# Hybrid conv and pooling layers on one core: fewer weights split ahead, a third GpSimd tile cut at tap 20, and buffers for the first norm's squares

## The chip, the core and the metric

The kernel runs on one core of one Trainium2 chip. Its engines are TensorE (PE in the rows; PEld is its weight load), VectorE (DVE), ScalarE (ACT), GpSimd (POOL) and SyncE (SP), whose queue issues the transfers here. Each engine carries out its own instructions in the order in which the program lists them, and waits where an operand or a buffer is not ready. The metric is the device time of one launch in microseconds; before the change it is 744.97 us, the median of three runs.

## The reference

Two layers act on a latent stream x of 1024 tokens by 1024 channels. Neither layer needs the context stream (only a later kind of layer reads it). Both are gated by a condition c.

```python
# each layer: modulated RMS norm, mixer, gated residual
sh, sc, gt = split(silu(c) @ w_mod[i] + b_mod[i], 3)
h = rms(x, norm_g[i]) * (1 + sc) + sh
x = x + gt * mixer_i(h)

def conv_mixer(h):                      # layer 0
    a, b, g = split(h @ w_in, 3)
    y = a * sigmoid(b)
    y = depthwise_conv(y, dw, 31 taps, same padding) + db
    y = silu(layernorm(y, ln_g, ln_b)) * silu(g)
    return y @ w_out

def pool_mixer(h):                      # layer 1
    v, g = split(h @ w_in, 2)
    pooled = [window_mean(v_k, w) for k, w in enumerate((2, 4, 8, 16))] - v
    y = (grouped 256x256 matmuls of pooled) * scale
    return (y * silu(g)) @ w_out
```

All arrays are float32.

## The kernel before

Channels lie on the 128 partitions, tokens along the free dimension. Every 1024 x 1024 product is made of eight output tiles of 128 channels (`ct` or `m`), each a sum over eight input tiles (`kt`), for two halves of 512 tokens (`h`; in layer 1 the parts are 504 and 520 tokens).

*Products in three passes.* Each float32 operand is split into a high part in fp32r (`hi_part`, L166 and L167, on ACT) and the rest (`lo_part`, L171 and L172, on DVE, or on GpSimd where `eng=nc.gpsimd`). `mm3` (L221 to L223) adds high x high, high x low and low x high. So a group of one output tile and one half is 24 matmuls. A weight is loaded into one of four `raw` buffers and split into two of four `w` tiles; so two split weights can be there at a time, and the next cast waits until the group two before it has been used.

*Layer 0.* After the input and its norm, tiles `a` and `b` are made for `y`. The depthwise convolution (`conv`, `conv_taps`) takes 31 taps for each tile and half. For most tiles DVE accumulates in PSUM (L524). For the tiles in `POOL_CT` ACT multiplies (L511, into one of two `pr` buffers) and GpSimd adds to `z` (L512), tap by tap: two tiles in half 0, five in half 1. The gates `g` (names `wg<ct><h>`, `psg`, `sgw`) fill TensorE while the convolution goes on and while the norm is computed; they are stored in DRAM (`sgd`) and come back as `sgr`.

*Weights split ahead.* `split_ahead` loads weights of layer 1 (`wk<i>`), splits them on ACT and GpSimd and stores the parts in DRAM (`keep`, names `kw<i>`). `load_pl` later loads such parts instead of splitting again (`load_kept`), or loads and splits the weight on ACT and DVE where none are kept. Each such weight is 512 KB, its two parts 1 MB.

*Norm and output.* `layernorm(h)` sums the eight `z` tiles on TensorE (`mr`), spreads the mean (`mu`), subtracts it on DVE, squares on ACT (`sqz`) and sums the squares on TensorE (`vpz`). For half 0 `square_sums` (L296) streams one column against each block of the square; for half 1 `quarter_sums` (L311) streams the square against 32 columns of ones. Squares lie in two `sq` buffers. `rstd_rows` makes the power on GpSimd (L268) and spreads it (`rbz`). `gate_norm` makes `y1`, and `out_half` the output product (`pso`), the residual and the sums for layer 1's norm (`vpy`, `rby`). `h2_half` makes layer 1's input (`h20`, L660 on DVE, L167 on ACT, L172 on DVE).

*What sets the order.* The program is written once and a scheduler orders the instructions of each engine by their priorities and a model of their times. `behind([...])` keeps what is issued inside it behind the given instructions in their engine's order, without a wait. `conv` has a low priority, so its taps fill gaps. In half 1 the tiles 4 to 7 are issued inside `behind([h2_done])`, where `h2_done` is DVE's last `lo_part` of layer 1's input.

*The second half's gates.* `gate_g(ct, (0, 1))` in the loop over `FILL` and `CORD[:2]` makes both halves of gates 0 and 2 with one load; gates 1 and 3 keep their weight (`wg_last`) and make half 1 after `layernorm(0)`; gates 4 to 7 load theirs again while layer 1's input is made.

Of the kernel before, what the change touches and what calls it, by code (L numbers as in the profile page):

```python
# [17 lines left out]
KT = 8  # L18
# [8 lines left out]
CORD = [ct for p in PAIRS for ct in p]  # L27
FILL = (4, 6, 5, 7)
MIX_AT = 4
ASIDE = (2, 3, 10, 11, 4, 5, 12, 13, 6, 7, 14, 15)  # L30
AT = (2, 2, 2, 2, 2, 2)
EARLY_W = (1, 1, 2, 2)
EARLY_AT = (0, 2, 1, 1)
EARLY_ENG = ((0, 0, 0, 0), (1, 1, 1, 1))
# [2 lines left out]
HOLD = (4, 2, 3, 4)  # L37
LAST = 2
MID_OUT = 6
TAIL = 8  # L40
NA = HW - TAIL
NB = L - NA
# [13 lines left out]
def hybrid_kernel(ctx, tc, xT, vecs, wm, wk, cv_first, cv_w, cv_wo, pl_w, pl_grp, pl_wo, out):  # L56
# [29 lines left out]
    def half(tag, name, dt=F32, cols=HW):  # L86
        return S.tile([P, WIDTH.get(tag, HW)], dt, tag=tag, name=name, bufs=RINGS[tag])[:, :cols]
# [4 lines left out]
    def bank(tag, name):  # L92
        return PS.tile([P, HW], F32, tag=tag, name=name, bufs={"mm": 5, "ax": 1, "cv": 2}[tag])
# [7 lines left out]
    def hs(h):  # L101
        return slice(h * HW, (h + 1) * HW)
# [4 lines left out]
    def packed(tags, name):  # L107
        res = []
        for j, tag in enumerate(tags):
            u = unit(tag, f"{name}{j}")  # L110
            res += [u[:, hs(0)], u[:, hs(1)]]
        return res
# [51 lines left out]
    def hi_part(hi, src, add=None):  # L164
        if add is None:
            return nc.scalar.copy(hi, src)  # L166
        return nc.scalar.activation(hi, src, AF.Identity, bias=add)  # L167
# [15 lines left out]
    @contextmanager  # L183
    def behind(instructions):
        with ExitStack() as stack:
            for i in instructions:
                stack.enter_context(tc.issue_after(i.ins))
            yield
# [104 lines left out]

        return (sums, None), add

    def square_sums(xs, name, vp):  # L296


        def add(i):
            sq = half("sq", f"sq{name}{i}")  # L300
            done = nc.scalar.activation(sq, xs[i], AF.Square)
            for j in range(4):
                nc.tensor.matmul(
                    vp[:, j : j + 1], sq[:, bl(j)], ones[:, 0:1], start=i + j == 0, stop=i == KT - 1,
                    skip_group_check=True,
                )
            return done

        return (None, vp), add

    def quarter_sums(xs, name, vp):  # L311


        def add(i):
            sq = half("sq", f"sq{name}{i}")
            done = nc.scalar.activation(sq, xs[i], AF.Square)
            for j in range(4):
                nc.tensor.matmul(
                    vp[32 * j : 32 * j + 32, :P], ones[:, :32], sq[:, bl(j)], start=i == 0, stop=i == KT - 1
                )  # L320
            return done

        return ("quarters", vp), add
# [36 lines left out]
    xs = [None, None]  # L360
# [106 lines left out]
    gt0, sh1, a1, gt1 = (const.tile([P, KT], F32, name=n) for n in ("gt0", "sh1", "a1", "gt1"))  # L467
# [19 lines left out]
    def conv(h, ct, taps=None, count=None):  # L487

        with priority(LATER * (1 + h)):
            for _ in islice(taps or conv_taps(h, ct), count):  # L490
                pass
# [59 lines left out]
    def gate_g(ct, halves, after=(), start=KT // 2, wg=None):  # L551
        wg = wg or gate_w(ct, halves[0])
        for h in halves:
            ps = mmps(f"psg{ct}{h}")
            gemm(ps, wg, hT[h], after, start)
            s = half("sg", f"sgw{ct}{h}")
            nc.scalar.activation(s, ps, AF.Silu)
            i = CORD.index(ct)
            nc.sync.dma_start(out=sgd[h][i // 2][:, hs(i % 2)], in_=s)
# [4 lines left out]

    aside = list(ASIDE)
    for i, ct in enumerate((*FILL, *CORD[:2])):
        split_ahead(AT[i])
        gate_g(ct, (0,) if ct in FILL else (0, 1))
    wg_last = {ct: gate_w(ct, 0) for ct in CORD[2:4]}
    for ct in CORD[2:4]:  # L570
        gate_g(ct, (0,), wg=wg_last[ct])
# [3 lines left out]
    def layernorm(h):  # L575
        z = [zs[h][ct] for ct in CORD]
        sums = axps(f"mr{h}")
        row = S.tile([P, HW], F32, tag="row", name=f"mrow{h}", bufs=1)
        mu = axps(f"mu{h}")
        with priority(-LATER):  # L580
            for i, ct in enumerate(ZORD[h]):
                g = slice(32 * (i % 4), 32 * (i % 4) + 32)
                nc.tensor.matmul(sums[g, :], onesd[:, :32], zs[h][ct], start=i < 4, stop=i >= 4)
            nc.scalar.copy(row, sums)
            last = nc.tensor.matmul(mu, selm, row, start=True, stop=True)
        sums_done[h] = last
        total, add = (square_sums, quarter_sums)[h](z, f"z{h}", bank(("ax", "cv")[h], f"vpz{h}"))
        for i in range(KT):
            nc.vector.tensor_tensor(out=z[i], in0=z[i], in1=mu, op=ALU.subtract)
            with priority(-LATER):  # L590
                squared[h] = add(i)
        return z, *rstd_rows(total, f"z{h}")
# [28 lines left out]
    def out_half(h, y1, ws, done, beside=None):  # L621
# [27 lines left out]
            finish(m, ps)  # L649
        return x1, total  # L650

    def h2_half(h, x1, total, region, first):
        rb, rb_done = rstd_rows(total, f"y{h}")
        res = []
        for kt in range(KT + 1):
            if kt < KT:
                if kt % 2 == 0:
                    u = pair(region, first + kt, f"h2{h}{kt}")
                x = x1[kt]
                mul = nc.vector.scalar_tensor_tensor(  # L660
                    out=x, in0=x, scalar=a1[:, kt : kt + 1], in1=rb, op0=ALU.mult, op1=ALU.mult
                )
                if kt:
                    ordered(mul)
                else:
                    started = mul
                res.append(cut(u, hs(kt % 2)))
                hi_part(res[kt][0], x, sh1[:, kt : kt + 1])
            if kt:
                end = ordered(lo_part(*res[kt - 1], x1[kt - 1], sh1[:, kt - 1 : kt]))  # L670
        return res, started, end, rb_done
# [1 line left out]
    ws = [load_split(cv_wo[m], f"wo0{m}", ("Q", 2 * m), eng=nc.gpsimd) for m in range(3)]  # L673
    conv(1, 0)
    z, rb, rb_done = layernorm(0)
    gate_g(CORD[2], (1,), wg=wg_last[CORD[2]])
    gate_g(CORD[3], (1,), [rb_done], HOLD[0], wg_last[CORD[3]])
    y1, done = gate_norm(0, z, rb)
    conv(1, 1)
    conv(1, 3)  # L680
# [1 line left out]
    x1, total = out_half(0, y1, ws, done)  # L682
# [8 lines left out]
    h2_0, h2_started, h2_done, rb_done = h2_half(0, x1, total, "Q", 0)  # L691
# [159 lines left out]
    for g in range(4):  # L851
        group = layer1_group(g, 0, h2_0, early, group if g else None)
        if g == 0:
            with behind([h2_done]):
                for ct in range(4, KT):
                    conv(1, ct)
        if g:
            ahead += [load_split(pl_wo[m], f"wp{m}0", ("E", 2 * m)) for m in ((0,), (1,), (2, 3))[g - 1]]
    with priority(-LATER):
        z, rb, rb_done = layernorm(1)  # L860
    layer1_out(0, range(MID_OUT - 1), ahead, group)
    with behind(spread_done):
# [12 lines left out]
    x1, total = out_half(1, y1, ws, done, beside)  # L875
    h2_1, _, _, rb_done = h2_half(1, x1, total, "Y", 2)
# [57 lines left out]
```

## Time and profile before

| | |
|---|---|
| median of three runs | 744.97 us (744.68 to 745.39) |
| the profiled execution | 746.58 us, span of its instructions 744.8 us |
| TensorE | 718.7 us busy (96%) |
| DVE, GpSimd, ACT | 506.1, 452.4, 386.6 us busy |
| granted TensorE clock | 0.997 of full speed over the span |
| moved through DMA | 130.86 MB |

In the rows below, a timeline row gives start and length in us, the engine, the line, the operation, output<-input by the program's names with buffer numbers left out, and in brackets the idle time before it with what ended it. "x8" means that many instructions in a row, merged into one length. Matmul lengths overlap, since matmuls are pipelined; their starts tell the pace. The fp32 matmuls of the sums are recorded as two passes each.

### The profile page before, as it was taken

What the parts mean: (1) busy time and instruction counts of PE and PEld (TensorE: products, weight loads), DVE (VectorE), ACT (ScalarE), POOL (GpSimd) and SP (SyncE); (2) the same over time, 40 slices, a digit from 0 to 9 for tenths busy, and PEclk for the clock granted to TensorE, in tenths of its full rate; (3) what the DMA queues carried; (4) which work ended last, traced back from release to release, by engine and by line L of the source; (5) the groups of instructions that cost most, each with busy time, mean ns of one, the idle gap of its engine ahead of it and who ended that gap; (6) DMA issues with size and microseconds to landing.
All of it is one profiled execution on the core that took longest, in us unless ns stands there. A gap on an engine that the chain in (4) does not pass through costs nothing.

```text
span 744.8 us, 9979 instructions
## 1 busy us (share of the span) xinstructions
PE 718.7 (96%) x3574; PEld 568.7 (76%) x3574; DVE 506.1 (68%) x712; ACT 386.6 (52%) x577; POOL 452.4 (61%) x389
## 2 busy tenths in 40 slices
PE   3899999999999999999989999999999999999998
PEld 1677787676776788878756887778887888888997
DVE  6997998789899770579859976352646464377321
ACT  5365456656656575876776773353434432443110
POOL 2000889999999999899999992044217423343231
PEclk9999999999999999999999999999999999999999
DMA  8882006465788974543662165365725511234142
GB/s 323 323 325 83 0 1 248 154 249 210 276 343 288 336 301 183 190 139 110 210 215 83 57 218 192 141 222 192 237 95 207 186 47 42 86 114 142 57 130 73
DMA packets 43394, 130.86 MB, mean 176 GB/s; under 512 B 4816, under 2 KB 6992, under 8 KB 43344
## 3 DMA queue, kind: packets, MB, share of 16 engines
q1 hardware_dynamic: 43344, 130.22, 49.5%
q8 instruction: 28, 0.46, 0.2%
q14 instruction: 22, 0.18, 0.1%
HBM read 105.04 MB, written 25.17 MB: 175 GB/s over the span
## 4 chain that ended last, share of the span: by engine, by line
PE 73%; POOL 10%; DMA 7%; DVE 5%; ACT 2%; issue 2%; SPq 0%; POOLq 0%; DVEq 0%; ACTq 0%
POOL z L512 9%; PE psv L223 4%; PE psv L222 4%; PE psf L223 4%; PE psf L221 4%; PE psq L223 4%; PE psf L222 4%; PE psv L221 4%; PE psq L222 4%; PE psq L221 4%; PE ps L221 3%; PE ps L223 3%; PE ps L222 3%; PE psg L223 3%; PE psg L221 2%; PE psg L222 2%
## 5 line engine op out<-in xcount | busy, mean ns | idle before, releaser
L512 POOL TENSOR_TENSOR z<-z,pr 128x512 f32<-128x512 f32 (+8 forms) x210 | 292.0, 1392 | 35.0 <-ACT z L508 14.9
L511 ACT ACTIVATE pr<-y,VT 128x512 f32<-128x512 f32 (+8 forms) x210 | 150.2, 720 | 93.3 <-POOL z L512 88.4
L524 DVE SCALAR_TENSOR_TENSOR cv<-y,VT,cv 128x512 f32<-128x512 f32 (+9 forms) x261 | 175.2, 742 | 0.3
L820 DVE SCALAR_TENSOR_TENSOR xf<-psf,gt,xf 128x260 f32<-128x260 f32 (+1 forms) x24 | 13.3, 570 | 41.2 <-PE psf L223 37.1
L268 POOL TENSOR_TENSOR vrx<-vex,mhalf 128x4 f32<-128x4 f32 x2 | 2.1, 1026 | 56.2 <-ACT vex L266 56.2
L803 DVE SCALAR_TENSOR_TENSOR q<-psy,VT,q 128x260 f32<-128x260 f32 (+1 forms) x24 | 13.6, 571 | 30.8 <-PE psy L223 30.6
L613 DVE TENSOR_TENSOR z<-z,rbz 128x512 f32<-128x512 f32 x16 | 10.7, 679 | 30.1 <-PE rbz L274 30.1
L716 DVE TENSOR_TENSOR s<-v 128x535 f32<-128x535 f32 x8 | 12.3, 1538 | 19.5 <-ACT v L769 19.5
L166 ACT CAST y<-q 128x504 fp32r<-128x504 f32 (+1 forms) x16 | 9.9, 620 | 24.2 <-DVE q L803 24.2
L327 DVE SCALAR_TENSOR_TENSOR wmb<-wmb,s_row 128x1024 f32<-128x1024 f32 x16 | 19.3, 1218 | 0.0
L714 DVE TENSOR_TENSOR s<-v,psv 128x512 f32<-128x512 f32 x8 | 5.5, 682 | 20.1 <-ACT v L769 20.1
L339 PE MATMUL gv<-wk,srep 128*32 128x256 f32 x256 | 18.6, 388 | 0.0
L729 POOL TENSOR_TENSOR s<-s,ecol 128x1 f32<-128x1 f32 (+5 forms) x14 | 4.4, 311 | 22.5 <-DVE s L720 22.5
L720 DVE TENSOR_TENSOR s<-s 128x517 f32<-128x517 f32 (+5 forms) x24 | 17.5, 731 | 0.6
L629 DVE SCALAR_TENSOR_TENSOR xr<-pso,gt,xr 128x512 f32<-128x512 f32 x16 | 11.6, 743 | 8.1 <-PE pso L223 8.1
L605 ACT ACTIVATE gn<-z,VT 128x512 f32<-128x512 f32 x16 | 12.4, 776 | 9.2 <-DVE z L613 9.0
L529 DVE TENSOR_TENSOR z<-z,cv 128x512 f32<-128x512 f32 x9 | 6.2, 685 | 15.0 <-ACT z L528 15.0
L223 PE MATMUL psy<-pd,grs 128*128 128x260 f32 (+1 forms) x48 | 15.3, 319 | 0.0
L222 PE MATMUL psy<-pd,grs 128*128 128x260 f32 (+1 forms) x48 | 15.2, 318 | 0.0
L221 PE MATMUL psy<-pd,grs 128*128 128x260 f32 (+1 forms) x48 | 15.2, 320 | 0.0
L769 ACT COPY v<-psv 128x512 f32<-128x512 f32 x16 | 9.3, 582 | 10.4 <-PE psv L223 10.2
L171 DVE TENSOR_TENSOR y<-q,y 128x504 fp32r<-128x504 f32 (+1 forms) x16 | 12.1, 756 | 3.7 <-ACT y L166 3.7
(2509 smaller groups left out, 2366.1 us busy)
## 6 DMA issues: line engine op xcount, KB each, us to landing
wk<-in_wk SPq DMA_DIRECT2D x32, 512.0 KB, 5.5
wmb<-in_wm SPq DMA_DIRECT2D x16, 512.0 KB, 6.7
wo<-in_cv_wo SPq DMA_DIRECT2D x16, 512.0 KB, 3.8
wp<-in_pl_wo SPq DMA_DIRECT2D x16, 512.0 KB, 3.5
wk<-in_pl_w SPq DMA_DIRECT2D x12, 512.0 KB, 5.9
wg<-in_cv_w SPq DMA_DIRECT2D x12, 512.0 KB, 5.0
x<-in_xT SPq DMA_DIRECT2D x16, 256.0 KB, 6.3
w<-in_cv_first SPq DMA_DIRECT2D x8, 512.0 KB, 6.4
```

Of the source, the lines that this page charges most:

```text
L221: nc.tensor.matmul(ps, w[0], r[0], start=first, stop=False)
L222: nc.tensor.matmul(ps, w[0], r[1], start=False, stop=False)
L223: nc.tensor.matmul(ps, w[1], r[0], start=False, stop=last)
L327: nc.vector.scalar_tensor_tensor(out=w, in0=w, scalar=1.0, in1=s_row, op0=ALU.mult, op1=ALU.mult, accum_out=out)
L339: nc.tensor.matmul(ps[32 * q : 32 * q + 32, :256], srep[:, kt, :], w[:, 256 * q : 256 * q + 256], start=kt == 0, stop=kt == KT - 1,)
L511: nc.scalar.activation(pr[:, o], y[:, i], AF.Copy, scale=dw(k))
L512: nc.gpsimd.tensor_tensor(out=z[:, o], in0=z[:, o], in1=pr[:, o], op=ALU.add)
L524: nc.vector.scalar_tensor_tensor(out=a[:, o], in0=y[:, i], scalar=dw(k), in1=a[:, o], op0=ALU.mult, op1=ALU.add)
L605: last = nc.scalar.activation(b, z[i], AF.Silu, scale=vcol(CORD[i], V_LG), bias=vcol(CORD[i], V_LB))
L720: nc.vector.tensor_tensor(out=s[:, :m], in0=s[:, :m], in1=s[:, step : step + m], op=ALU.add)
L803: mixed[0] = nc.vector.scalar_tensor_tensor(out=sg[m][:, piece], in0=ps, scalar=vcol(ct, V_PS), in1=sg[m][:, piece], op0=ALU.mult, op1=ALU ...
L820: nc.vector.scalar_tensor_tensor(out=xt[:, piece], in0=ps, scalar=gt1[:, m : m + 1], in1=xt[:, piece], op0=ALU.mult, op1=ALU.add)
```

## The change

Eight weights are split ahead instead of twelve (`ASIDE` loses 6, 7, 14 and 15; they are split in layer 1 when they are needed), at other places in the loop (`AT`). Gates 0 and 2 are made for half 0 only in that loop; their half 1 follows the norm with a second load, split on ACT and DVE. The first norm's squares are summed with `quarter_sums` like the second's, and five of its eight squares get buffers of their own. In half 1 the tiles 5 to 7 are no longer issued behind DVE's last `lo_part` (which only ordered DVE); tile 6 is issued up to tap 20, and its rest, and so tile 7, behind the eight casts of layer 1's input (`h2_his`, on ACT).

```diff
-ASIDE = (2, 3, 10, 11, 4, 5, 12, 13, 6, 7, 14, 15)
-AT = (2, 2, 2, 2, 2, 2)
+ASIDE = (2, 3, 10, 11, 4, 5, 12, 13)
+AT = (1, 2, 2, 2, 1, 0)
...
+TAPS_AHEAD = 20
...
-    def quarter_sums(xs, name, vp):
+    def quarter_sums(xs, name, vp, homes=()):
...
-            sq = half("sq", f"sq{name}{i}")
+            sq = homes[i] if i < len(homes) else half("sq", f"sq{name}{i}")
...
         split_ahead(AT[i])
-        gate_g(ct, (0,) if ct in FILL else (0, 1))
+        gate_g(ct, (0,))
...
-        total, add = (square_sums, quarter_sums)[h](z, f"z{h}", bank(("ax", "cv")[h], f"vpz{h}"))
+        vp = bank(("ax", "cv")[h], f"vpz{h}")
+        if h:
+            total, add = quarter_sums(z, f"z{h}", vp)
+        else:
+            homes = packed(["Q6", "Q7"], "sqz") + [half("vs", "sqz4")]
+            total, add = quarter_sums(z, f"z{h}", vp, homes)
...
-                hi_part(res[kt][0], x, sh1[:, kt : kt + 1])
+                his.append(hi_part(res[kt][0], x, sh1[:, kt : kt + 1]))
...
-    gate_g(CORD[2], (1,), wg=wg_last[CORD[2]])
-    gate_g(CORD[3], (1,), [rb_done], HOLD[0], wg_last[CORD[3]])
+    for ct in CORD[2:4]:
+        gate_g(ct, (1,), wg=wg_last[ct])
+    gate_g(CORD[0], (1,))
+    gate_g(CORD[1], (1,), [rb_done], HOLD[0])
...
             with behind([h2_done]):
-                for ct in range(4, KT):
-                    conv(1, ct)
+                conv(1, 4)
+            conv(1, 5)
+            taps = conv_taps(1, 6)
+            conv(1, 6, taps, TAPS_AHEAD)
+            with behind(h2_his[0]):
+                conv(1, 6, taps)
+            conv(1, 7)
```

On GpSimd, between the gate weights wg6 and wg2 of the first half, there stood (`z` rows are taps of tile 3 in half 1, `wk` rows are low parts of weights split ahead, `wg` rows low parts of gate weights):

```order
L171 TENSOR_TENSOR wg60l<-wg_2046,wg60h 128x1024
L171 TENSOR_TENSOR wk13l<-wk_2144,wk13h 128x1024
L512 TENSOR_TENSOR z_2683<-z_2683,pr_2794 128x512
L171 TENSOR_TENSOR wg50l<-wg_2100,wg50h 128x1024
L512 TENSOR_TENSOR z_2683<-z_2683,pr_2797 128x512
L171 TENSOR_TENSOR wk6l<-wk_2188,wk6h 128x1024
L171 TENSOR_TENSOR wg70l<-wg_2154,wg70h 128x1024
L512 TENSOR_TENSOR z_2683<-z_2683,pr_2800 128x512
L171 TENSOR_TENSOR wk7l<-wk_2198,wk7h 128x1024
L171 TENSOR_TENSOR wg00l<-wg_2208,wg00h 128x1024
L512 TENSOR_TENSOR z_2683<-z_2683,pr_2803 128x512
L171 TENSOR_TENSOR wk14l<-wk_2270,wk14h 128x1024
```

Now there stand, from wg6 on in the same place:

```order
L172 TENSOR_TENSOR wg60l<-wg_2036,wg60h 128x1024
L514 TENSOR_TENSOR z_2656<-z_2656,pr_2767 128x512
L172 TENSOR_TENSOR wk12l<-wk_2134,wk12h 128x1024
L514 TENSOR_TENSOR z_2656<-z_2656,pr_2770 128x512
L172 TENSOR_TENSOR wg50l<-wg_2090,wg50h 128x1024
L172 TENSOR_TENSOR wk13l<-wk_2178,wk13h 128x1024
L514 TENSOR_TENSOR z_2656<-z_2656,pr_2773 128x512
L172 TENSOR_TENSOR wg70l<-wg_2144,wg70h 128x1024
L514 TENSOR_TENSOR z_2656<-z_2656,pr_2776 128x512
L172 TENSOR_TENSOR wg00l<-wg_2188,wg00h 128x1024
L514 TENSOR_TENSOR z_2656<-z_2656,pr_2779 128x512
L514 TENSOR_TENSOR z_2656<-z_2656,pr_2782 128x512
```

wk12's low part, which stood ahead of wg6's, is now behind it; wk6, wk7, wk14 and wk15 are gone. After one more tap wg2's low part follows.

On TensorE, in the gates of the first half, the squares' sums (`vpz`) stood in four places of two squares each; this is the first, between the last matmuls of gate 0 and the first of gate 2:

```order
L221 MATMUL psg_2242<-h16h,wg00h 128x512
L222 MATMUL psg_2242<-h16l,wg00h 128x512
L303 MATMUL vpz_2495<-ones,sqz_2497 128x1 x4
L303 MATMUL vpz_2495<-ones,sqz_2504 128x1 x4
L223 MATMUL psg_2242<-h16h,wg00l 128x512
L221 MATMUL psg_2296<-h00h,wg20h 128x512
```

Now seven of the eight squares stand in one place, between gates 2 and 1 of half 0:

```order
L224 MATMUL psg_2228<-h06h,wg20l 128x512
L320 MATMUL vpz_2399<-sqz_2400,ones 32x128 x8
L320 MATMUL vpz_2399<-sqz_2401,ones 32x128 x8
L320 MATMUL vpz_2399<-sqz_2402,ones 32x128 x4
L320 MATMUL vpz_2399<-sqz_2434,ones 32x128 x4
L320 MATMUL vpz_2399<-sqz_2441,ones 32x128 x4
L222 MATMUL psg_2268<-h00h,wg10h 128x512
```

The order of the operands and the shape have changed with the form; the eighth square comes two matmuls into gate 3.

On ACT, where layer 1's input is cast (`h20`), the products of the taps (`pr`) stood between the casts:

```order
L511 ACTIVATE pr_3729<-y_1662,VT 128x508
L557 ACTIVATE sgw_3374<-psg_3349 128x512
L511 ACTIVATE pr_3732<-y_1662,VT 128x507
L511 ACTIVATE pr_3735<-y_1662,VT 128x506
L167 ACTIVATE h200h<-xr_2901,sh_625 128x512 x2
L511 ACTIVATE pr_3738<-y_1662,VT 128x505
L511 ACTIVATE pr_3741<-y_1662,VT 128x504
L167 ACTIVATE h202h<-xr_2902,sh_625 128x512
L511 ACTIVATE pr_3744<-y_1662,VT 128x503
L557 ACTIVATE sgw_3408<-psg_3383 128x512
L167 ACTIVATE h202h<-xr_2902,sh_625 128x512
```

Now the eight casts follow each other, with one gate (`sgw`) among them:

```order
L513 ACTIVATE pr_3702<-y_1662,VT 128x508
L559 ACTIVATE sgw_3347<-psg_3322 128x512
L168 ACTIVATE h200h<-xr_2874,sh_625 128x512 x2
L168 ACTIVATE h202h<-xr_2875,sh_625 128x512 x2
L559 ACTIVATE sgw_3381<-psg_3356 128x512
L168 ACTIVATE h204h<-xr_2876,sh_625 128x512 x2
L168 ACTIVATE h206h<-xr_2877,sh_625 128x512 x2
L513 ACTIVATE pr_3705<-y_1662,VT 128x507
L513 ACTIVATE pr_3708<-y_1662,VT 128x506
```

The products of tile 6 from 128x507 on, and all of tile 7, are behind the casts.

## Rows read from the trace of the kernel before

**Rows 1.** The page: busy us, share of the span and instructions of each engine.

```profile
PE 718.7 (96%) x3574; PEld 568.7 (76%) x3574; DVE 506.1 (68%) x712; ACT 386.6 (52%) x577; POOL 452.4 (61%) x389
```

**Rows 2.** What TensorE waited for: us in total, times, longest us.

```profile
PE psg L223 <- DVE wg51l L171: 1.4, 1, 1.4
PE psv L221 <- ACT h200h L167: 1.3, 1, 1.3
...
PE psg L223 <- POOL wg60l L171: 1.1, 1, 1.1
PE psv L222 <- DVE h200l L172: 0.7, 1, 0.7
PE psg L221 <- ACT wg51h L166: 0.7, 1, 0.7
...
PE psg L223 <- DVE wg61l L171: 0.5, 1, 0.5
...
PE vpy L303 <- ACT sqy L301: 0.3, 1, 0.3
```

**Rows 3.** Busy us by stretch: length, PE, PEld, DVE, ACT, POOL, granted clock, DMA.

```profile
220.00:260.00 40.00, 38.69 (x169) 28.47 (x168) 33.59 (x54) 23.81 (x32) 38.94 (x21) 1.00 0.87 301
392.00:396.00 4.00, 3.69 (x9) 2.93 (x10) 4.00 (x6) 3.49 (x6) 3.36 (x6) 0.58 0.68 270
451.00:500.00 49.00, 49.00 (x262) 37.38 (x262) 27.30 (x41) 20.57 (x36) 9.38 (x18) 1.00 0.51 180
```

**Rows 4.** Timeline of TensorE around two squares of the first norm.

```profile
275.41 0.39 PE L223 MATMUL psg<-h06h,wg20l 128*128 128x512 f32 x1
...
275.64 1.84 PE L303 MATMUL vpz<-ones,sqz 128*128 128x1 f32 x16
...
277.66 0.39 PE L222 MATMUL psg<-h06l,wg20h 128*128 128x512 f32 x1
```

**Rows 5.** Timeline of TensorE around two squares of the second norm.

```profile
468.53 0.39 PE L222 MATMUL psq<-h204l,wq50h 128*128 128x512 f32 x1
...
468.85 0.65 PE L318 MATMUL vpz<-sqz,ones 128*32 128x128 f32 x16
...
469.76 0.40 PE L221 MATMUL psq<-h206h,wq50h 128*128 128x512 f32 x1
```

**Rows 6.** Timeline of DVE: the first norm's subtractions.

```profile
259.93 4.86 DVE L589 TENSOR_TENSOR z<-z,mu 128x512 f32<-128x512 f32 x8
```

**Rows 7.** Timeline of GpSimd: taps (L512) and a split (L171).

```profile
245.17 1.31 POOL L512 TENSOR_TENSOR z<-z,pr 128x512 f32<-128x512 f32 x1
246.42 2.42 POOL L171 TENSOR_TENSOR wk6l<-wk,wk6h 128x1024 fp32r<-128x1024 f32 x1
...
323.96 52.11 POOL L512 TENSOR_TENSOR z<-z,pr 128x512 f32<-128x512 f32 x31 [0.91 <-ACT pr L511]
...
400.50 11.62 POOL L512 TENSOR_TENSOR z<-z,pr 128x500 f32<-128x500 f32 x8
```

**Rows 8.** Timeline of ACT: wg5's cast and the casts of layer 1's input.

```profile
373.38 0.73 ACT L511 ACTIVATE pr<-y,VT 128x512 f32<-128x512 f32 x1 [1.68 <-POOL z L512]
374.01 1.03 ACT L166 CAST wg51h<-wg 128x1024 fp32r<-128x1024 f32 x1
...
389.06 0.72 ACT L511 ACTIVATE pr<-y,VT 128x506 f32<-128x506 f32 x1 [0.64 <-POOL z L512]
389.68 1.32 ACT L167 ACTIVATE h200h<-xr,sh 128x512 fp32r<-128x512 f32 x2
...
401.65 0.72 ACT L167 ACTIVATE h206h<-xr,sh 128x512 fp32r<-128x512 f32 x1 [0.36 <-DVE xr L660]
```

**Rows 9.** Timeline of TensorE: rby, the end of wg7's group, a sum.

```profile
382.94 1.12 PE L274 MATMUL rby<-dgy,ones 128*128 128x512 f32 x2
...
388.77 0.39 PE L223 MATMUL psg<-h16h,wg71l 128*128 128x512 f32 x1
...
453.66 1.05 PE L583 MATMUL mr<-z,onesd 128*32 128x512 f32 x4
```

More of the change, by code (lines that the diff above doesn't have):

```diff
@@ L294, in squares, with square_sums @@
         return (sums, None), add
-    def square_sums(xs, name, vp):
+    def square_sums(xs, name, vp, homes=()):
         def add(i):
-            sq = half("sq", f"sq{name}{i}")
+            sq = homes[i] if i < len(homes) else half("sq", f"sq{name}{i}")
             done = nc.scalar.activation(sq, xs[i], AF.Square)
@@ L309, in square_sums @@
         return (None, vp), add
-    def quarter_sums(xs, name, vp):
+    def quarter_sums(xs, name, vp, homes=()):
         def add(i):
-            sq = half("sq", f"sq{name}{i}")
+            sq = homes[i] if i < len(homes) else half("sq", f"sq{name}{i}")
             done = nc.scalar.activation(sq, xs[i], AF.Square)
@@ L650, in out_half @@
         return x1, total
+    h2_his = []
     def h2_half(h, x1, total, region, first):
         rb, rb_done = rstd_rows(total, f"y{h}")
-        res = []
+        res, his = [], []
+        h2_his.append(his)
         for kt in range(KT + 1):
```

## The prediction

> **What bounds the kernel now.** I read the page's busy times first: TensorE is busy for 718.7 of 744.8 us, GpSimd for 452.4 [rows 1]. So the end is set by the sum of what TensorE streams and by the moments in which it waits; an edit counts if it shortens one of the two. Next comes the view of TensorE's waits [rows 2]. Outside the start of the kernel, which the change leaves alone, and one wait near 574 us, it names seven that matter here, all between 238 and 393 us: 1.1 us for the low part of wg6 from GpSimd; 0.5 + 0.3 + 0.7 + 1.4 = 2.9 us for wg6 and wg5 of the second half and a square; 1.3 + 0.7 = 2.0 us for the first tile of layer 1's input. Then the busy time by stretch [rows 3]: in 220 to 260 us GpSimd is busy 38.94 of 40 us, so who waits for a weight there waits for GpSimd's queue; in 392 to 396 us the granted clock is 0.58, the only low stretch after the start, and it follows the 2.0 us wait; in 451 to 500 us DVE (27.3 of 49) and ACT (20.6) have room. Then the timelines around the edited places [rows 4 to 9].
>
> **Term 1, the sums of squares of the first norm (TensorE).** Both forms have 32 matmuls, each recorded as two passes. In the old form two squares stand between the matmul at 275.41 and the one two places later at 277.66: 2.25 us; without them it would be two steps of 0.23, so they cost 2.25 - 0.46 = 1.79 [rows 4]. In the new form, which the second norm already has, 468.53 to 469.76 is 1.23, less 0.46 is 0.77 [rows 5]. Eight squares are four such pieces: 7.2 before, 3.1 after; seven of the eight now stand in one piece, which saves joints, and a 128x4 matmul comes in (at 0.2). I take 2.9 for the new form: **-4.2 us**. Bounds: -3.9 (joints as before) and -4.4. No cover is involved: TensorE has no idle time in this stretch. But the squares must be there when the block of 28 matmuls comes up, since TensorE runs in order. With five new homes ACT no longer waits for a square's buffer. The mean now comes out a little under 258 us; eight subtractions on DVE of 0.6 follow [rows 6], and each square follows its subtraction on ACT in a pass of 0.7 [rows 8]; eight of these after the first subtraction end at 258 + 0.6 + 8 x 0.7 = 264.2, so seven are ready by 266. The block stands behind the wg2 group and comes at about 267.8: 1.8 us early.
>
> The Trainium skill, "TensorE: Matmul & The Clock Gate", section "LDWEIGHTS (loading the stationary operand)", says that a weight load takes its column count divided by 1.2 ns, and the section before it gives a gap of N / 2.4 + 2.5 ns. An estimate from that page is 64 x 107 ns = 6.8 us for the old form and 64 x 56 = 3.6 for the new: -3.3, and the forecast would be 735.3. In the trace the old passes come to 1.84 / 16 = 0.115 us, as it says [rows 4]; the new ones to 0.65 / 16 = 0.041, under the page's figure [rows 5]. Both forms are measured in this kernel, so the rows decide, and that sum gets no chance of its own.
>
> **Term 2, weights of the first gates (GpSimd, then TensorE).** Four of the weights split ahead go, 2.42 us of GpSimd each = 9.7 us [rows 7], with their stores and their later loads. wg6's low part now stands ahead of wk12's in GpSimd's row, so it comes one split (2.4) earlier than a wait of 1.1 needs: **-1.1 us**. In return wg0 and wg2 are used for one half only: TensorE spends 24 x 0.23 = 5.5 us on each weight instead of 11, and asks for the following ones sooner. GpSimd's new row from wg6 to wg2 costs, with 2.42 a split and 1.31 a tap [rows 7]: to wg5 7.5, to wg7 6.2, to wg0 3.7, to wg2 6.4, in all 23.7 us. TensorE takes 4 x 5.5 = 22.1 for four groups, and 1.05 each for a last sum and the mean [rows 9]: 24.2. It keeps pace; marched through with these durations, the tightest is wg7 with some 0.3 us. Bounds: +3.6 (six weights late by 0.6, half a split-and-tap of queueing) to -0.2 more; I take +0.4 of small lateness.
>
> **Term 3, the waits around 367 to 377 us.** They belong to ACT: the cast of wg5 at 374.01 stands behind a product (pr) that waited 1.68 us for a GpSimd tap [rows 8]. GpSimd has no pause there: 31 taps in 52.1 us [rows 7]. The change puts GpSimd ahead by 9.7 us of splits, less one tap more in front of the same cast (1.3) and a new wait at the first norm's power, taken as 1: 7.4 us. Two new DVE splits (the second halves of wg0 and wg2, loaded again) lie beside taps.
>
> There the Trainium skill, "SBUF — State Buffer", section "Who interferes with whom", speaks against the change: a DVE instruction with two SBUF operands keeps GpSimd's reads out while it lasts. The trace bears it out in size: a tap takes 1.31 in 245 us, but 52.11 / 31 = 1.68 where DVE makes low parts [rows 7]. By that rule the two cost GpSimd up to 2 us more, and term 3 with it (a rival below).
>
> Without that loss GpSimd leads TensorE by 7.4 - 4.2 - 1.1 = 2.1 us. TensorE cannot lose these waits faster than ACT comes forward, so of the 2.9 us go **-2.0 us**. Bounds: 0 (the lead is used up where ACT waits for TensorE's outputs) and -2.9.
>
> **Term 4, layer 1's input.** The casts h2 stood in ACT's row between products that wait for GpSimd; now all eight come first, and taps 20 to 30 of tile 6 and all of tile 7 behind them. rstd's spread (rby) ends at 384.06; a DVE product and a cast of 0.7 each [rows 8] could give h200h by 386, and TensorE wants it at 388.77 + 0.39 = 389.16 [rows 9]. It began at 389.68, right behind the product at 389.06 [rows 8]. Over 2 us early instead of 1.3 late: **-2.0 us**, and the low clock that followed goes: (1 - 0.58) x 4 = **-1.7 us** [rows 3]. Bounds: 0, and -3.7 for both.
>
> **What is late next.** GpSimd now waits during the casts, and 41 taps remain instead of 33. Call the end of wg7's group P (389.16 before). The eighth cast ended 12.7 us after the first began (389.68 to 402.37) [rows 8]; free of products it is there by P + 10 at the latest. 41 taps at 1.46 (8 in 11.62 [rows 7]) end at P + 70. TensorE asks for the last two tiles in the second norm's sum, which the change moves back from between the matmuls of wv5 at 453.66 [rows 9] to behind two thirds of wq5's: 468.76 before (just ahead of the squares of [rows 5]); less 389.16, less the waits and low clock of term 4 (3.7) and the sum and mean that now come later (2.1), P + 74. So 4 us are left. The last four weights of layer 1's first part are now split by ACT and DVE instead of loaded split: 4 x 1.03 and four DVE splits of like size, in 451 to 500 us, where both have 20 us to spare [rows 3]. At nothing; with that cover gone, 1 us per weight.
>
> **Sum.** -4.2 - 1.1 - 2.0 - 2.0 - 1.7 + 0.4 = -10.6. The profiled execution took 746.58, so 736.0 by it; it stands 1.6 above the median of 744.97, and against that the forecast is **734.4 us**. Its own range is 732.4 (all waits gone: -4.4 - 1.3 - 2.9 - 3.7 = -12.3, rounded outwards) to 737.
>
> **Rivals.** *Taps held up by DVE:* a tap beside DVE's splits takes 1.68 on average, 0.4 more than alone [rows 7], and single ones more; with the two new splits costing GpSimd 2 us, its lead of 2.1 is gone, and term 3 with it: 734.4 + 2.0 = **736.4**. For it: the same 31 taps; against it: the two fall where DVE is otherwise little loaded. (It is the rule of the SBUF page above.)
> *Weights just late:* with groups of 5.5 us a cast of 1.03, a tap of 1.31 and a split of 2.42 must fit behind the freed buffer: 4.8, and with wk13, wo00 or wo01 ahead in the row it does not. For it speaks that wg7 has 0.3 us; against it that GpSimd's total is below TensorE's. 734.4 + 1.1 + 3.6 = **739.1**.
> *Only the sums pay:* GpSimd's lead ends where ACT waits for TensorE, ACT stays as late as it was, and terms 2 to 4 are lost: 745.0 - 4.2 = **740.8**. Against it: the removed products in front of h200h are in no way a matter of lead.
> *GpSimd too late for the second norm (slower):* every us by which the 41 taps pass P + 74 is TensorE's at the sum. It starts at (74 - 10) / 41 = 1.56 us a tap, not far over 1.46, and eats all gain at 1.56 + 10.6 / 41 = 1.82. Taps beside low parts took 1.68 on average [rows 7], which costs 5 us: 739. If every tap came to 2.2, it would be 734.4 + 41 x 0.64 = **760.6**. For it: the 8 taps moved, and the pause; against it: DVE makes few splits behind the casts.
>
> **How the numbers follow.** Forecast 0.56; taps held up 0.10; weights late 0.13; only sums 0.07; GpSimd late 0.14, of it 0.06 around 1.8 us a tap, within 0.2% of before (1.5 us, about what a measurement of this kernel can tell from no change), and 0.08 slower. Faster 0.86, same 0.06, slower 0.08. From 732.4 to 741 lie the first four cases, 0.86.
>
> **What would show it.** Right: a block of 28 matmuls for the squares near 268 us, 2.2 us long, and no wait at wg6; h200h not waited for and a full clock through 380 to 400 us; GpSimd idle some 10 us there; its last tap before TensorE's second sum. Wrong: TensorE waits for wg7, wg2 or wg1 (term 2), for the squares (term 1), for wg5 of the second half with GpSimd no earlier than TensorE (term 3), or at the second norm's sum for a tile of GpSimd (the last rival).

## The result, and the profile after

The changed kernel takes 736.58 us (median of 4 runs, 735.97 to 738.9) against 744.86 (4 runs, 744.68 to 745.39): a ratio of 0.989, with a 95% interval of 0.9874 to 0.9905. That is 8.3 us faster. The forecast was 734.4 with a range of 732.4 to 741.0, so the direction and the range held and the size was 2.2 us too large. The profiled execution took 736.21, and for it the working had given 736.0. Both facts have to be explained: why the two profiles agree with the working so well, and why the medians do not.

The page's busy times first; the columns are those of [rows 1].

```profile
PE 712.1 (97%) x3576; PEld 561.8 (76%) x3576; DVE 512.8 (70%) x718; ACT 388.1 (53%) x580; POOL 444.5 (61%) x385
```

TensorE has lost 6.6 us of busy time and the span 10.4, from 744.8 to 734.4. What TensorE waited for, against [rows 2] (us in total, times, longest), without the start:

```profile
PE psg L224 <- DVE wg51l L172: 1.4, 1, 1.4
...
PE psg L222 <- ACT wg51h L167: 0.5, 1, 0.5
PE psv L224 <- DVE wv60l L172: 0.5, 1, 0.5
PE pso L224 <- POOL wo17l L172: 0.5, 1, 0.5
```

The waits for wg6 in both halves, for the square and for layer 1's input are gone. That for wg5 of the second half has stayed at 1.9 us, and one for wv6 has come. The stretches that answer to [rows 3] (length, then busy us of PE, PEld, DVE, ACT, POOL, granted clock, DMA):

```profile
220.00:260.00 40.00, 40.00 (x178) 30.17 (x178) 35.30 (x57) 25.37 (x35) 39.20 (x23) 1.00 0.76 262
...
384.00:388.00 4.00, 4.00 (x19) 3.25 (x18) 3.87 (x7) 2.34 (x4) 0.10 (x1) 1.00 0.67 266
451.00:500.00 49.00, 48.46 (x252) 34.69 (x251) 26.35 (x36) 24.71 (x39) 21.43 (x20) 1.00 0.61 204
```

TensorE no longer pauses between 220 and 260 us, and in the stretch behind layer 1's input the clock is full and GpSimd idle (0.10 of 4 us). Next TensorE's timeline at the first norm's squares, which answers to [rows 4]:

```profile
266.65 0.39 PE L224 MATMUL psg<-h06h,wg20l 128*128 128x512 f32 x1
266.96 1.74 PE L320 MATMUL vpz<-sqz,ones 128*32 128x128 f32 x56
268.63 0.50 PE L222 MATMUL psg<-h00h,wg10h 128*128 128x512 f32 x1
268.96 0.39 PE L223 MATMUL psg<-h00l,wg10h 128*128 128x512 f32 x1
```

The block of 28 matmuls (56 passes) stands at 266.96, where 267.8 was expected, and takes 268.63 - 266.65 - 0.23 = 1.75 us. ACT had the seven squares ready, as its timeline shows; the seventh ends at 264.37, where the prediction had all eight by 264.2:

```profile
258.59 3.22 ACT L318 ACTIVATE sqz<-z 128x512 f32<-128x512 f32 x6
...
263.75 0.62 ACT L318 ACTIVATE sqz<-z 128x512 f32<-128x512 f32 x1
```

GpSimd's timeline around the second half's weights and at its last tap, against [rows 7]:

```profile
315.63 52.03 POOL L514 TENSOR_TENSOR z<-z,pr 128x512 f32<-128x512 f32 x31 [0.90 <-ACT pr L513]
...
451.57 2.24 POOL L514 TENSOR_TENSOR z<-z,pr 128x497 f32<-128x497 f32 x1
```

The 31 taps are as slow as before (52.03 against 52.11 us) but begin 8.33 us earlier. The last tap ends at 453.81. TensorE's second sum begins at 454.08, as the next row shows, and with it two of the pieces in which the second norm's squares now stand:

```profile
454.08 1.05 PE L585 MATMUL mr<-z,onesd 128*32 128x512 f32 x4
...
476.92 0.43 PE L320 MATMUL vpz<-sqz,ones 128*32 128x128 f32 x8
...
479.57 0.43 PE L320 MATMUL vpz<-sqz,ones 128*32 128x128 f32 x8
```

Eight pieces of one square each have taken the place of four pairs of 0.65 [rows 5].

### The profile page after: what moved, and what is told of

It is laid out like the page before. It is cut to its first block, busy times and chain, and to the rows that moved or that the text cites. A ratio compares the mean times of both kernels' runs of the same rounds, so it can differ in the third digit from the quotient of the medians.

```text
span 734.4 us, 9975 instructions
## 1 busy us (share of the span) xinstructions
PE 712.1 (97%) x3576; PEld 561.8 (76%) x3576; DVE 512.8 (70%) x718; ACT 388.1 (53%) x580; POOL 444.5 (61%) x385
## 4 chain that ended last, share of the span: by engine, by line
PE 82%; DVE 9%; POOL 3%; issue 2%; ACT 2%; DMA 1%; SPq 0%; POOLq 0%; DVEq 0%; ACTq 0%
PE ps L222 4%; PE ps L223 4%; PE ps L224 4%; PE psf L222 4%; PE psf L224 4%; PE psf L223 4%; PE pso L224 4%; PE pso L222 4%; PE pso L223 4%; PE psv L224 4%; PE psg L224 4%; PE psv L223 4%; PE psg L222 4%; PE psv L222 4%; PE psg L223 3%; PE psq L223 3%
## 5 line engine op out<-in xcount | busy, mean ns | idle before, releaser
L172 POOL TENSOR_TENSOR wo14l<-wo,wo14h 128x1024 fp32r<-128x1024 f32 x1 | 2.4, 2410 | 23.1 <-ACT wo14h L167 23.1
L801 ACT ACTIVATE q<-psq 128x512 f32<-128x512 f32 x16 | 9.5, 592 | 8.8 <-DVE y L172 5.1
```

What stands on the lines that cost most here:

```text
L172: return eng.tensor_tensor(out=lo, in0=src, in1=hi.bitcast(F32), op=ALU.subtract)
```

## The experiments

All times are medians. The unchanged kernel took 744.9 to 745.4 in the three studies. "Ratio" is to it, with the 95% interval.

| run | what it is | us | ratio |
|---|---|---|---|
| e0_again | before, unchanged | 744.87 | 0.9991 to 1.0013 |
| e1_sums | before + sums | 742.69 | 0.9955 to 0.9979 |
| e2_weights | before + weights | 743.89 | 0.9979 to 0.9998 |
| e3_taps | before + taps | 743.12 | 0.9961 to 0.9985 |
| e4_nosums | weights + taps | 742.65 | 0.9960 to 0.9984 |
| e5_noweights | sums + taps | 742.40 | 0.9946 to 0.9971 |
| e6_notaps | sums + weights | 740.23 | 0.9920 to 0.9950 |
| (the change) | all three | 736.58 | 0.9874 to 0.9905 |
| e8_order | change, gates in the old order | 737.40 | 0.9883 to 0.9909 |
| e9_twelve | change, twelve weights ahead | 740.31 | 0.9918 to 0.9948 |
| e7_homes2 | change + homes for the second norm | 736.80 | 0.9872 to 0.9900 |
| e10_ring | change + wg5 out of the ring | 738.33 | 0.9892 to 0.9921 |
| e11_best | e7 + e10 + GpSimd splits | 739.07 | 0.9905 to 0.9930 |

**The kernel before, once more.** Nothing is edited.

> The kernel before, unchanged. The profiled execution of it took 746.58 us, the median 744.9; its profile shows the granted clock at 0.58 for 4 us behind the wait at layer 1's input. Theory 1: that low stretch (1.7 us) belongs to some executions only, so the timed ones have a mean clock of 0.999 and a span near 743.1, and 1.7 us of my term 4 were never in the median. Theory 2: all executions have the low stretch, and the 1.6 us lie around the span: spans of 744.8 with a clock of 0.997 and 743.1 + 1.8 does not fit.

This profile took 744.08 us. Its stretches at the start, behind the wait for wg5 of the second half, and behind layer 1's input:

```profile
12.00:16.00 4.00, 1.87 (x8) 1.78 (x8) 3.30 (x7) 1.20 (x2) 0.80 (x1) 0.50 1.02 418
...
376.00:380.00 4.00, 3.48 (x9) 2.75 (x10) 3.83 (x3) 2.66 (x6) 3.92 (x3) 0.59 0.59 200
...
392.00:396.00 4.00, 4.00 (x19) 3.26 (x18) 4.00 (x6) 3.20 (x6) 3.35 (x6) 1.00 0.57 227
```

and two of its waits:

```profile
PE psv L222 <- DVE h200l L172: 0.7, 1, 0.7
...
PE psg L223 <- POOL wg60l L171: 0.3, 1, 0.3
```

Here the clock is at 1.2 GHz (0.50) from 12 to 24 us, where TensorE is idle about half of the time, and at 2.4 GHz (1.00) at layer 1's input, where only 0.7 us is waited for, none of it for h200h. The wait for wg6 is 0.3 instead of 1.1. A low stretch of 4 us (0.59) is there in this execution too, but at 376 us, behind the 2.1 us waited for wg5. TensorE loses 1.4 us in it and ends wg7's group at 389.45 + 0.39 = 389.84 (389.16 in the first profile), so that h200h is ready when it comes: the loss takes the place of the wait of 1.3 us. Of the 35 executions of this kernel in the study, the three with a mean clock of 1.000 spanned 742.4 to 743.0 us, and the five at 0.997, the figure of the profile that the prediction was read from, 744.1 to 744.8. Theory 1 stands in the main: the low clock behind layer 1's input belongs to some executions, and by their spans most lose little or nothing to it.

**One part alone.** The three parts are hunks of the change that can be applied one by one. Sums:

```diff
-        total, add = (square_sums, quarter_sums)[h](z, f"z{h}", bank(("ax", "cv")[h], f"vpz{h}"))
...
+            homes = packed(["Q6", "Q7"], "sqz") + [half("vs", "sqz4")]
+            total, add = quarter_sums(z, f"z{h}", vp, homes)
```

> Only the new form of the first norm's sums with its five homes; weights and taps as before. Theory A (the terms add): TensorE is 4.7 to 5.4 us shorter there, 739.5 to 740.2. Theory B (one chain): between 367 and 392 us TensorE waits for ACT, whose row stands behind GpSimd's taps, and these do not come earlier; so what the sums save is waited for there again: 743 to 745, with waits of 8 to 10 us for wg6 and wg5 of the second half and for h200h instead of 4.9.

Weights:

```diff
-ASIDE = (2, 3, 10, 11, 4, 5, 12, 13, 6, 7, 14, 15)
-AT = (2, 2, 2, 2, 2, 2)
+ASIDE = (2, 3, 10, 11, 4, 5, 12, 13)
+AT = (1, 2, 2, 2, 1, 0)
...
-        gate_g(ct, (0,) if ct in FILL else (0, 1))
+        gate_g(ct, (0,))
...
+    gate_g(CORD[0], (1,))
+    gate_g(CORD[1], (1,), [rb_done], HOLD[0])
```

> Only the shorter list of weights split ahead and the new order of the gates; sums and taps as before. Theory A: wg6 and wg5 no longer waited for (-1.3), about -1.0 at 367 to 370 us, +0.5 for a weight of layer 1 that DVE now splits: 743.1. Theory B: GpSimd is 9.7 us of splits ahead and TensorE hardly earlier, so ACT comes forward and all waits from 367 to 392 us (4.9 us) but the one for wg5 of the second half (2.0) go: 744.9 - 1.3 - 2.9 + 0.5 = 741.2.

Taps:

```diff
-                for ct in range(4, KT):
-                    conv(1, ct)
+                conv(1, 4)
+            conv(1, 5)
+            taps = conv_taps(1, 6)
+            conv(1, 6, taps, TAPS_AHEAD)
+            with behind(h2_his[0]):
+                conv(1, 6, taps)
+            conv(1, 7)
...
```

> Only GpSimd's third tile from tap 20 on behind the casts of layer 1's input; sums and weights as before. Both theories: the two waits at layer 1's input (1.9 us) go: 743.0; waits at 238 and at 367 to 377 us stay. Rival: 41 taps behind the casts make GpSimd late for the second norm's sum and TensorE waits there: 745 or more.

The taps did what was expected: 1.8 us, at 743.12. The sums brought 2.2 of the 4.7 to 5.4, nearer to theory B, but the waiting is at a place that neither theory had named: TensorE waits 3.0 us in all for y1 and wo03, nearly all of it for their casts on ACT, between 311 and 326 us. The weights brought 1.0; both theories had more, and instead of the waits at wg5 there are 3.0 us at wg6 of the second half. What TensorE waited for with the sums alone, and then with the weights alone:

```profile
PE psg L223 <- DVE wg51l L171: 1.4, 1, 1.4
PE pso L221 <- ACT y102h L166: 1.4, 2, 1.0
PE pso L221 <- ACT wo03h L166: 0.8, 1, 0.8
```

```profile
PE psg L221 <- ACT wg61h L166: 1.6, 1, 1.6
PE psg L223 <- DVE wg61l L171: 1.4, 1, 1.4
PE pso L221 <- ACT wo03h L166: 1.2, 1, 1.2
```

The single gains add to 2.2 + 1.0 + 1.8 = 5.0 us, and the whole change brings 8.3. The parts need each other. From here on I held a theory of two rows: TensorE's own work, and GpSimd's splits and taps, behind which ACT's casts stand. The later of the two sets the pace up to layer 1, so shortening one alone is waited out.

**One part left out.** The same hunks, taken back one at a time from the changed kernel; in the last one that is:

```diff
-            taps = conv_taps(1, 6)
-            conv(1, 6, taps, TAPS_AHEAD)
...
+                for ct in range(4, KT):
+                    conv(1, ct)
```

> The changed kernel with the old form of the first norm's sums; weights and taps as changed. Theory of two rows (TensorE's and that of GpSimd with ACT, of which the later sets the end; either alone shortened is waited out): weights and taps alone give about their single gains, 744.9 - 1.0 - 1.8 = 742.1. Theory of terms that add, with the 1.7 us that I read off the changed kernel for the second norm's squares, which stand there one by one and here in pairs again: 736.6 + 5.4 - 1.7 = 740.3.

> The changed kernel with the old list of weights split ahead and the old order of the gates; sums and taps as changed. Two rows: GpSimd is as late as before, so the sums' gain is waited out in ACT's casts of y1 near 311 to 322 us, as in the run with the sums alone: 744.9 - 2.2 - 1.8 = 740.9. Terms that add: 736.6 + 1.3 + 1.0 - 0.5 - 1.7 = 736.7, no slower than the changed kernel.

> The changed kernel with all taps of layer 0 as before; sums and weights as changed. Two rows: sums and weights together make up the whole that the single runs lack (744.9 - 2.2 - 1.0 - 3.3 = 738.4), waits at y1's casts absent. Rival: the surplus hangs on the taps: 744.9 - 2.2 - 1.0 = 741.7. By my term 4 the waits at layer 1's input come back: 736.6 + 1.9 = 738.5, up to 740.3 with the low clock.

Without the sums 742.65, as two rows have it (742.1, or 742.6 counted from this study's 745.35); terms that add (740.3) are out by more than the interval. Without the weights 742.40: 5.8 us are lost, terms that add said 736.7, and two rows 740.9, which is also 1.5 too little. Without the taps 740.23, inside the span that my term 4 gave (738.5 to 740.3), but between the two rows' 738.4 and the rival's 741.7. Its executions at a mean clock of 1.000 took 739.06 and 739.38, those at 0.995 took 741.95 and 742.7. The profile, one of these, shows two low stretches: the clock at 0.58 in the 4 us behind the waits for h200h and h200l, and at 0.82 and 0.75 behind a wait of 1.1 us for wv6:

```profile
384.00:388.00 4.00, 3.81 (x10) 2.99 (x11) 4.00 (x6) 3.47 (x6) 3.35 (x6) 0.58 0.56 222
...
464.00:468.00 4.00, 2.79 (x15) 1.76 (x16) 1.84 (x2) 3.88 (x6) 0.75 (x1) 0.82 0.87 318
468.00:472.00 4.00, 4.00 (x15) 3.19 (x14) 1.82 (x2) 1.05 (x1) 0.00 (x0) 0.75 0.60 209
```

So sums and weights together bring 745.35 - 740.23 = 5.1 where they bring 2.2 and 1.0 apart, and no cast of y1 is waited for. That is the sign of the theory, but the surplus is 1.9 where it had 3.3. The rest hangs on the taps, as the rival has it: they bring 740.23 - 736.58 = 3.6 on top of the other two, and 1.8 alone.

The theory also leaves out the order. Of ACT's products for the taps, 158 stand ahead of the cast of wg6 for the second half before the change, 157 with the sums alone, 159 in the whole change, but 165 with the weights alone and without the sums. With the sums alone, that cast starts at 364.32 us, hardly sooner than before (364.77): GpSimd's row has not come forward. With the weights alone it starts at 367.83, later than before: GpSimd is rid of four splits, but the scheduler has put seven more taps ahead of the cast. Every edit makes the scheduler choose another order, and no run holds the order fixed. So how much of the surplus comes from the length of the rows, and how much from the order, is not shown.

**What in the weights part is it.** The part has two halves, the shorter list and the order of the gates. With the sums alone, DVE stood 5.71 us for the gates of tiles 1 and 3 to come back from DRAM, so the order, which computes these earlier, was a rival cause. DVE's timeline there:

```profile
307.35 0.70 DVE L613 TENSOR_TENSOR gn<-gn,sgr 128x512 f32<-128x512 f32 x1 [5.71 <-DMA sgr<-sgd]
```

The first run keeps the list of eight and restores the order; the second keeps the order and restores the list of twelve.

```diff
-        gate_g(ct, (0,))
+        gate_g(ct, (0,) if ct in FILL else (0, 1))
...
-    gate_g(CORD[0], (1,))
-    gate_g(CORD[1], (1,), [rb_done], HOLD[0])
...
```

> The changed kernel, list of eight weights and all else kept, but the gates of the first two tiles for both halves at once, as before, so that those of tiles 1 and 3 are computed 11 us later. Theory of the gates' way: in the run with the sums alone DVE waited 5.71 us for the gates of tiles 1 and 3 to come back from DRAM (4.50 with sums and taps); with the norm 8 us earlier the same wait of 4 to 6 us stands here, y1's casts come no sooner and the time is 741 to 742.4. Theory of two rows (GpSimd's splits are what held ACT back): eight weights are enough, no such wait decides, 736.6 to 738.

```diff
-ASIDE = (2, 3, 10, 11, 4, 5, 12, 13)
-AT = (1, 2, 2, 2, 1, 0)
+ASIDE = (2, 3, 10, 11, 4, 5, 12, 13, 6, 7, 14, 15)
+AT = (2, 2, 2, 2, 2, 2)
```

> The changed kernel with twelve weights split ahead (two in front of each of the six groups) and the new order of the gates. Theory of the gates' way: no wait for the gates in DVE's row; GpSimd's 9.7 us more of splits make the low parts of wg7 to wg1 late instead, since TensorE takes 5.5 us a group and GpSimd 6 to 7.5: six groups late by 0.5 to 1.5 each, about 740. Theory of two rows: GpSimd is as late as in the run without the weights part, 742.4.

With the old order the wait for the gates is there again in DVE's timeline:

```profile
303.51 0.70 DVE L615 TENSOR_TENSOR gn<-gn,sgr 128x512 f32<-128x512 f32 x1 [4.71 <-DMA sgr<-sgd]
```

and yet the kernel takes 737.40, 0.8 more than the change, with intervals that overlap. A wait of 4.7 us on DVE was covered but for 0.6 us of TensorE's at y103. The theory of the gates' way falls for this kernel. Twelve weights cost 3.7 us (740.31). The price was the one expected, but its places were only partly: not six late groups, but two (wg6 and wg5, 0.7 together), the squares (0.9 + 0.4, as TensorE came to their block before they were ready), wg1 (0.5) and, largest, wg6 of the second half. The waits of that run:

```profile
PE psg L224 <- DVE wg61l L172: 2.0, 1, 2.0
PE vpz L320 <- DVE z L596: 0.9, 1, 0.9
...
PE psg L222 <- ACT wg10h L167: 0.5, 1, 0.5
PE psg L224 <- POOL wg60l L172: 0.5, 1, 0.5
```

So the list is worth most of the part: 3.7 us with the new order, and 742.40 - 737.40 = 5.0 with the old one. The order is worth 0.8 with eight weights. With twelve it is worth about 2, from 742.40 (sums and taps, both parts of the weights as before) to 740.31, and there the 2.1 us of waits for y1 and wo03 go with it: with twelve weights the order is not little.

**What is left: the second norm's squares, wg5, wv6.** First homes for the second norm as well, in buffers that are free by then:

```diff
...
+        homes = packed([["Q6", "Q7"], ["Y6", "Y7"]][h], f"sqz{h}") + [half("vs", f"sqz{h}4")]
+        total, add = quarter_sums(z, f"z{h}", vp, homes)
```

> The changed kernel, with five homes for the second norm's squares too, so that six of them stand in one piece in TensorE's row instead of eight pieces of one. Theory: the single pieces cost 1.7 us against pairs (0.55 in their own rows, the rest in the matmuls beside them), and a block wins that and a little more: 736.6 - 1.9 = 734.7. Rival 1: only what the squares' own rows show comes back: 736.6 - 0.6 = 736.0. Rival 2: TensorE waits for the squares, since the block asks for the last of them sooner: 736.6 or more.

736.80, no change. From wg7's end to 566 us its trace is 0.6 us shorter than the change's, not 1.9. Six squares do stand in one piece, but TensorE comes to it too early and goes at ACT's pace. TensorE's row of it, and ACT's:

```profile
472.84 2.69 PE L320 MATMUL vpz<-sqz,ones 128*32 128x128 f32 x48
```

```profile
472.35 2.71 ACT L318 ACTIVATE sqz<-z 128x512 f32<-128x512 f32 x5
```

Five squares take ACT 2.71 us, 0.54 each, and TensorE needs 1.75 / 7 = 0.25. Rival 2 named this wait, and it takes up most of what the joints give back.

Then wg5 of the second half in a buffer of its own, with layer 1's fourth early weight in the ring in its place:

```diff
-EARLY_W = (1, 1, 2, 2)
+EARLY_W = (1, 1, 2, 3)
...
+        w = gate_w(ct, 1, ("E", 6) if ct == FILL[2] else None)
...
-        slots = ("EQ"[part], 2 * k)
+        slots = ("EQ"[part], 2 * k) if part or k < 3 else None
```

> The changed kernel with wg5 of the second half in the buffers that the fourth early weight of layer 1 had, and that weight in the ring in its place and loaded one group later. Theory: wg5's cast waited for wg4's buffer of the ring (free when TensorE ends wg4's group at 359.75) and then behind two products, so this wait goes wherever TensorE goes; with a buffer of its own the cast comes two products sooner and the waits of 0.54 + 1.40 go: 736.6 - 1.9 = 734.7. Rival: it is GpSimd's lead over TensorE that is used up, so the same 1.9 us turn up at wg7 or at layer 1's input: 736.6.

738.33, no faster. The rival holds: wg5 is not waited for any more, and wg7 is; another 1.1 us come at a sum of the second half.

```profile
PE psg L222 <- ACT wg71h L167: 1.8, 1, 1.8
PE vpy L255 <- DVE vay L293: 1.1, 1, 1.1
```

ACT's timeline in this run shows why: wg5's cast has come forward to 361.82, but wg7's stands at 372.61 behind products that wait for GpSimd's taps (0.41 and 0.97 us).

```profile
361.82 1.03 ACT L167 CAST wg51h<-wg 128x1024 fp32r<-128x1024 f32 x1
...
370.28 0.72 ACT L513 ACTIVATE pr<-y,VT 128x511 f32<-128x511 f32 x1 [0.41 <-POOL z L514]
371.98 0.72 ACT L513 ACTIVATE pr<-y,VT 128x510 f32<-128x510 f32 x1 [0.97 <-POOL z L514]
372.61 1.03 ACT L167 CAST wg71h<-wg 128x1024 fp32r<-128x1024 f32 x1
```

Last all three edits, with GpSimd making the low parts of layer 1's last weights:

```diff
-        return load_split(pl_w[i], name, eng=nc.gpsimd if part and i % KT > 1 else nc.vector)
+        return load_split(pl_w[i], name, eng=nc.gpsimd if i % KT > (1 if part else 5) else nc.vector)
```

> The changed kernel with the ring's edit, with homes for the second norm's squares, and with layer 1's last four weights of the first part split by GpSimd instead of DVE. If the ring's edit pays 1.9, the homes the 0.7 that their trace showed from the end of wg7's group to 566 us, and GpSimd's splits the wait of 0.5 for wv6: 736.6 - 3.1 = 733.5. If the ring's wait only moves: 735.4.

739.07, no gain either: the wait at wg7 stays, and one of 2.5 us for wv7 has come, whose raw weight is still on its way when ACT is free. No version tried beats the change.

## Why the prediction was right, and where it was off

**The conversion to the median is the step that failed.** The sum of -10.6 was made against the profiled 746.58, from which its rows come, and gave 736.0 for an execution that took 736.21. Then 1.6 us were taken off again because the profile "stands 1.6 above the median". But this 1.6 was no overhead of profiling: the second profiled execution of the same kernel took 744.08. TensorE's steps in the two differ by 0.7 us at the wait for wg6 and by 1.6 us behind layer 1's input, where only the first has the low clock. These microseconds were counted as gains in terms 2 and 4 and subtracted once more; the taps alone, which are term 4, brought 1.8 by medians and not 3.7. Against the medians the forecast should have been -10.6 + 1.6 = -9.0, near 736.

That the sum meets the profile to 0.2 us is in part luck: term 3 was 1.1 too large and 1.8 of new cost stood at nothing, while terms 1, 2 and 4 were 1.3 too small, and 1.4 at the start and in single steps were not counted.

**The terms.** By TensorE's steps in the two profiles, from start to start of its matmuls (squares as the prediction measured them, to the second matmul behind each piece, with the 128x4 matmul):

| | forecast | the two profiles |
|---|---|---|
| 1, squares of the first norm | -4.2 | -4.5: 7.16 before, 2.63 after |
| 2, wg6 and the next weights | -1.1 + 0.4 | -1.3, none late |
| 3, 367 to 377 us | -2.0 of 2.9 | -0.9 |
| 4, waits and clock at layer 1's input | -2.0 - 1.7 | -1.9 - 2.2, with the steps beside the waits |
| the second norm's squares | 0 | +1.3 |
| low part of wv6 on DVE | 0 | +0.5 |

To the end of wg7's group the gain is 389.16 - 380.79 = 8.4 us, of it 0.3 from the start of the kernel, 2.2 of waits, 4.5 of squares and 1.3 in single steps beside waits and sums, which I don't resolve. By the wait for wo17 near 570 us it is 10.0, and 10.4 at the end.

*Term 1* was sized from pairs; a longer piece is cheaper still: 268.96 - 266.65 - 0.46 = 1.85 for seven is 0.26 a square, against 0.77 / 2 = 0.385. The 56 passes take 1.75 / 56 = 0.031 us each, while the weight load of one is recorded with 0.106 to 0.110 us. The Trainium skill, "TensorEngine Tiling (Array Packing)", section "Key Properties", says that different tiles can load weights and multiply in parallel; the trace agrees.

*Term 2* was right in size for that profile, and the cause is GpSimd's row: with twelve weights the waits for wg6 and wg5 are back (0.5 and 0.2).

*Term 3* was the wrong kind of sum. I took a lead of 7.4 us on GpSimd, subtracted what TensorE gains, and called the rest a gain. But where TensorE waits for a cast behind GpSimd's taps, its time is GpSimd's time: wg5's cast came 374.01 - 365.59 = 8.42 us earlier, GpSimd's 31 taps 8.33, and TensorE resumes there 8.4 us earlier. GpSimd and TensorE came forward alike, and TensorE still waits 1.9 us for wg5: that is the prediction's own sign that term 3 is wrong. Up to those taps GpSimd was busy 6.6 us less (9.7 for the four splits, less 1.3 for the tap, less 1.7 for the rival below) and idle 1.7 less. Terms 1 to 3 together were -6.9 in the forecast and are -8.4. The ring's run bears this out, since freeing wg5 moved the wait to the next cast in ACT's row.

*The rival of taps held up by DVE* came true in its cost and not in its consequence. The two new splits on DVE run from 282.1 and 294.67 us, 2.22 us each, well ahead of the 31 taps. One tap beside each, at 283.35 and 295.88 us, takes 2.14 and 2.13 us, and the others between 278 and 315 us take 1.3. So GpSimd loses 1.7 us, which is what the Trainium skill, "SBUF — State Buffer", section "Who interferes with whom", leads one to expect of a DVE instruction with two inputs in SBUF. The 31 taps themselves took no longer than before (52.03 against 52.11 us).

*Term 4* was right for that pair of profiles. By medians the taps are worth half of it when made alone (1.8), and 3.6 on top of the other two parts.

**What was late next.** GpSimd was idle 9.5 us beside the casts, near the 10 that were forecast. Then the 41 taps ran from 389.14 to 453.81, 1.58 us each with what lies between them, where I had 1.46 and had put the start of the slower rival at 1.56. The last tap ended 0.27 us ahead of TensorE's sum, not 4. So that rival did not come about, but only 0.27 us were left; what a later tap would have cost was not tried.

**What I had priced at nothing.** The second sum moved behind GpSimd's taps, and with it each square of the second norm came up by itself in TensorE's row. The order of instructions showed that before, and I didn't price it. In their own rows the eight single pieces take 0.55 us more than the four pairs, and each piece costs 0.2 at its joints: the step into it is 0.32 and the one after it 0.33 instead of 0.23. With four more pieces that makes 0.55 + 0.8, about 1.3. The Trainium skill, "TensorEngine Tiling (Array Packing)", section "Key Properties", says that a change of tiling mode drains TensorE; the steps agree. The split of wv6 on DVE was half covered: it cost 0.5 of the 1 us named for lost cover.

## What to carry to other kernels

Read the same kernel's profile more than once before pricing a wait from it, and never subtract the distance to the median when a term already contains its cause. Where a later wait hangs on another engine's row, gains ahead of it do not add: compute when each row arrives there and take the later one. Removing work from one row and from the other may each bring little, and both together much; but look first at what order the scheduler makes of each version, since it may spend the freed time on other work ahead of the same wait.

## What the runs showed of the hardware

One kernel's executions differ in where the clock falls. Behind waits of about 2 us in a full part of the unchanged kernel it falls for some 4 us, to 0.58 at 392 us in the first profile and to 0.59 at 376 in the second. At 392 us it costs 1.6 us of the span; at 376 it costs 1.4 us there, and a later wait of 1.3 goes. In the run without the taps two low stretches, at 384 us and from 464 to 472, go with about 3 us more.

The recorded clock of the start needs care. The second profile has 0.50 from 12 to 24 us and the first 1.00, but in the first too the matmuls up to 27 us start 0.43 us apart, as they do in the low stretch at 392 us, and 0.23 apart behind it:

```profile
25.74 0.63 PE L222 MATMUL pf<-h00l,w00h 128*128 128x512 f32 x1
26.17 0.63 PE L223 MATMUL pf<-h00h,w00l 128*128 128x512 f32 x1
```

So it fits that the 12 executions at a mean clock of 0.988, the mean of the second profile, span 742.3 to 743.5 but for one (745.4), hardly more than the 742.4 to 743.0 of those at 1.000; only one of the 12 was profiled. A mean granted clock without its place says little of the time.
